# Moving a quarter of the partial groups of an output projection into the norm stages

## The chip, the cores and the metric

The kernel runs on one core of a Trainium2 chip. The metric is the device time of one execution in microseconds (us). Three runs of the kernel before gave 2637.51, 2638.96 and 2642.91 us, a median of 2638.96 us. The engines are called PE (TensorE, the matrix engine), DVE (VectorE), ACT (ScalarE), POOL (GpSimd) and SP (SyncE, which here only issues transfers).

## The reference

The program is a decoder trunk of two layers over 1024 tokens of width 1024, in float32. Cut to what the change touches:

```
for layer in (0, 1):
    hn = rmsnorm(h, ln_mix_pre[layer])
    m  = o @ w_out              # layer 0: o = attention heads (1024 wide)
                                # layer 1: o = y * recurrent scan (1280 wide)
    h  = h + rmsnorm(m, ln_mix_post[layer])
    u  = rmsnorm(h, ln_mlp_pre[layer])
    h  = h + rmsnorm(square(relu(u @ w_up[layer])) @ w_down[layer], ln_mlp_post[layer])
    h  = h + rmsnorm(p[layer] @ w_proj, ple_norm) * sigmoid(h @ w_gate)
```

## The kernel before

**Products.** Each float32 product is done as three matmuls (`mm3`, L153): both operands are split in a high and a low part (`split`, L121: a cast on ACT, then a subtraction on DVE), and high*high, high*low and low*high are summed in PSUM. One block of 128 contraction rows against 512 columns is three matmuls of 128x512. A weight piece of 256 rows x 512 columns (512 KB) is loaded by SP into `wraw`, of which there are two buffers, and split from there into `wA`, `wB` or `wC` tiles (`stage`, L131).

**The output projection** `m = o @ w_out` is cut in two along the contraction. One part is done early, as soon as its rows of `o` exist, in 16 *partial groups*: a group takes one block of 128 tokens (`tb`, 0 to 7) and one half of the output columns (`nh`, 0 or 1), sums 4 contraction blocks (12 matmuls) in layer 0 and 6 (18 matmuls) in layer 1, is copied from PSUM by ACT into a tile `st`, and goes to a DRAM buffer `part[tb]`. In layer 0 the groups (`out_part`, L650) fill gaps of the last attention heads; the list `parts_` (L685) says how many at each step. In layer 1 (`out_partial`, L870, called at the end of the recurrent mixer with `any_bank`) they stand at the mixer's end and take turns on four PSUM banks: two named `tp`, one `mm`, one `av`. After them two rows of `o` are read back from DRAM (`hyD`) and split.

**The norm stage** (`Layer.mix_out`, L929) does the rest. For each token block `out_row` (L953) reads `part[tb]` into a tile `c`, multiplies the other four contraction blocks (24 matmuls, into one of three pairs of PSUM banks), adds the partial on DVE (`a<-sc,c`), and applies both norms. `combine` (L973) then transposes the normed block on PE (8 transposes into the two `tp` banks) and makes from it the operands of a Strassen-like scheme for the first MLP product: for the first four blocks only `B11` and `B21`, for the last four also the sums T1 to T4 and `B22`, with transposes, casts and subtractions on ACT and DVE. T2, T3 and T4 live in three pairs of tiles `x0`, `x1`, `x2` (`extra`, L932), which nothing uses before the second half of the combines. Six halves of the first MLP products ("leads", `None` in the plan) stand between. Below, R0 to R7 are the rows in the order in which they are done, K0 to K7 their combines.

**What sets the order.** The table `plan` (L1011) gives the order in which the steps are written; a scheduler of the framework then orders each engine's instructions by its own model of times. Each engine and each transfer queue works in its order: an instruction that waits holds what stands behind it.

Of the kernel before, what the change touches and what calls it, by code (L numbers as in the profile page):

```python
# [17 lines left out]
P = 128  # L18
# [21 lines left out]
def tile_hybrid_trunk(  # L40
# [283 lines left out]
    def mixer_attention(woD):  # L324
# [8 lines left out]
        with ExitStack() as cx:  # L333
# [319 lines left out]
            def out_part():  # L653
                ws = {}

                def group(nh, tb):
                    if nh not in ws:
                        ws[nh] = [stage_k(attn_w_out[0], 4 + 2 * i, 2, nh * 512, 512) for i in range(2)]
                    acc = bank("mm")
                    tok_group(acc, tb, lambda kb: (ws[nh][(kb - 4) // 2].h[:, kb % 2, :],  # L660
                                                   ws[nh][(kb - 4) // 2].l[:, kb % 2, :]), range(4, KB))
                    st = at.tile([P, 512], F32, name="st", bufs=2)
                    nc.scalar.copy(out=st, in_=acc)
                    nc.scalar.dma_start(out=woD[tb][:, nh * 512:(nh + 1) * 512], in_=st)

                return [lambda nh=nh, tb=tb: group(nh, tb) for nh in range(2) for tb in range(NT)]

            work_of = {b: block_work(order[n + 1]) if n + 1 < len(order) else
                       out_part() + [lambda tb=tb: ple(tb) for tb in range(NT)]
# [12 lines left out]
            ensure(units[0][1])  # L682
            setup_small(at)
            probs = {0: units[0][1].scores(0)}
            parts_ = [4, 3, 4, 4, 2, 2, 2, 1, 1, 1]  # L685
            for i, (blk, hd, g) in enumerate(units):
                work = work_of[blk]

# [178 lines left out]
    FACTOR = {"A11": B11, "A12": B21, "S2": T2, "S1": T1, "S3": T3, "A22": T4, "S4": B22}  # L867
    NLEAD = 3

    def out_partial(wap, kbs, kpairs, part, st_tile, pick_bank):  # L870

        ws = {}

        def group(nh, tb):
            if nh not in ws:
                ws[nh] = [stage_k(wap, r, 2, nh * 512, 512) for r in kpairs]
            acc = pick_bank()
            tok_group(acc, tb, lambda kb: (ws[nh][(kb - kbs[0]) // 2].h[:, kb % 2, :],
                                           ws[nh][(kb - kbs[0]) // 2].l[:, kb % 2, :]), kbs)
            st = st_tile()  # L880
            nc.scalar.copy(out=st, in_=acc)
            nc.scalar.dma_start(out=part[tb][:, nh * 512:(nh + 1) * 512], in_=st)

        return [lambda nh=nh, tb=tb: group(nh, tb) for nh in range(2) for tb in range(NT)]

    def vec(out, a, b, op):
        nc.vector.tensor_tensor(out=out, in0=a, in1=b, op=op)  # L887

# [22 lines left out]
    class Layer:  # L911
# [14 lines left out]
            return h  # L926


        def mix_out(self, wap, kpairs, src, part, order):  # L929
            layer, TA, TB = self.layer, self.TA, 1 - self.TA  # L930
            self.xpool = tc.alloc_tile_pool(name=f"ux{layer}", bufs=1, side="right", reuse_waits="tile")
            extra = [tuple(self.xpool.tile([P, 4, 512], F32R, name=f"x{x}{i}") for x in "hl")  # L932
# [6 lines left out]
            open_psum(f"ps_o{layer}")  # L939
            pairs[0] = 3  # L940
            with tc.tile_pool(name=f"pre{layer}", bufs=1, reuse_waits="tile") as mp:
                wslots.insert(0, (mp, "wBh", "wBl", 1, 1))
                wcount[0] = 0
                w = [[stage_k(wap, r, 2, nh * 512, 512) for r in kpairs] for nh in range(2)]
                gains = [mp.tile([P, D], F32, name="gain", bufs=2) for _ in range(2)]
                bcast_row(gains[0], ln_mix_post[layer:layer + 1, :])
                bcast_row(gains[1], ln_mlp_pre[layer:layer + 1, :])
                ready = {}

                def blocks(t):  # L950
                    return t.rearrange("p (k t) -> p k t", t=P)

                def out_row(tb):  # L953
                    a = mp.tile([P, D], F32, name="a", bufs=3)
                    pt = self.cpool.tile([P, D], F32, name=f"c{2 + tb % 2}", bufs=1)
                    nc.sync.dma_start(out=pt, in_=part[tb])
                    acc = pair_bank()
                    th, j = divmod(tb, 4)
                    sl = slice(j * P, (j + 1) * P)
                    for nh in range(2):  # L960
                        cs = slice(nh * 512, (nh + 1) * 512)
                        for kb in range(4):
                            lh, ll = U(th, kb)
                            mm3(acc[:, cs], lh[:, sl], ll[:, sl], w[nh][kb // 2].h[:, kb % 2, :],
                                w[nh][kb // 2].l[:, kb % 2, :], kb == 0, kb == 3)
                    vec(a, acc, pt, ALU.add)
                    junk = mp.tile([P, 512], F32, name="r").bitcast(BF16)
                    h = self.add_norm(tb, gains[0], a, a, src(tb), junk, mp)
                    nc.sync.dma_start(out=hD[tb], in_=h)
                    rs = rms_row(mp, a, h)  # L970
                    scale_gain(a, h, rs, gains[1])
                    ready[tb] = a

                def combine(tb):
                    n = ready.pop(tb)
                    th, j = divmod(tb, 4)
                    H, L = ([t[x][:, :, j * P:(j + 1) * P] for t in self.comb] for x in range(2))
                    ps = []
                    for kh in range(2):
                        tp = bank("tp")  # L980
                        for q in range(4):
                            kb = kh * 4 + q
                            nc.tensor.transpose(tp[:, q * P:(q + 1) * P], n[:, kb * P:(kb + 1) * P], ident)
                        ps.append(blocks(tp))
                    p1, p2 = ps
                    s = row_tile()
                    s1, s2 = (blocks(s[:, kh * 512:(kh + 1) * 512]) for kh in range(2))
                    if th == TA:
                        split(H[B11], L[B11], p1)
                        nc.scalar.copy(out=s1, in_=p1)  # L990
                        split(H[B21], L[B21], p2)
                        nc.scalar.copy(out=s2, in_=p2)
                        nc.sync.dma_start(out=self.uD[j], in_=s)
                        return
                    nc.sync.dma_start(out=s, in_=self.uD[j])
                    t2, t3 = (blocks(mp.tile([P, 512], F32, name="u", bufs=2)) for _ in range(2))
                    t1, t4 = s1, s2
                    vec(t1, p1, s1, ALU.subtract)
                    split(H[T1], L[T1], t1)
                    nc.scalar.copy(out=t3, in_=p1)  # L1000
                    vec(t2, p2, t1, ALU.subtract)
                    split(H[T2], L[T2], t2)
                    vec(t3, p2, t3, ALU.subtract)
                    split(H[T3], L[T3], t3)
                    vec(t4, s2, t2, ALU.subtract)
                    split(H[T4], L[T4], t4)
                    split(H[B22], L[B22], p2)

                a, b, c = (self.lead_steps(q, mp) for q in range(NLEAD))
                leads = [a[0], a[1], b[0], c[0], b[1], c[1]]  # L1010
                plan = [(out_row, 0), (out_row, 1), (out_row, 2), (combine, 0), (out_row, 3), (combine, 1),  # L1011
                        (out_row, 4), (combine, 2), (out_row, 5), (combine, 3), None, (combine, 4),
                        (out_row, 6), None, (combine, 5), (out_row, 7), None, None, (combine, 6), None,
                        lambda: self.early_sums(mp), (combine, 7), None]
                for step in plan:
                    if step is None:
                        leads.pop(0)()
                    elif callable(step):
                        step()
                    else:  # L1020
                        step[0](order[step[1]])
                del wslots[0]
# [435 lines left out]
    mixer_attention(parts[0])  # L1458

    m = Layer(0, 1, False)  # L1460
    m.mix_out(attn_w_out[0], (0, 2), lambda tb: x[0, tb * P:(tb + 1) * P, :], parts[0], (4, 5, 6, 7, 0, 1, 2, 3))
    m.mlp_and_ple()

    hyD = [dram.tile([P, S], F32, name=f"hyD{n}") for n in range(RB)]

    def rec_out(rp, wap, hyD):
        for f in out_partial(wap, range(2, KB), (2, 4, 6), parts[1],
                             lambda: rp.tile([P, 512], F32, name="st", bufs=2), any_bank):
            f()

    mixer_recurrent(hyD, rec_out)
    for n in range(2):
        t = row_tile()
        nc.sync.dma_start(out=t, in_=hyD[n])
        for th in range(2):
            split(*U(th, 2 + n), t[:, th * 512:(th + 1) * 512])
    m = Layer(1, 0, True)
    m.mix_out(rec_w_out[0], (8, 0), lambda tb: hD[tb], parts[1], (0, 1, 2, 3, 4, 5, 6, 7))
    m.mlp_and_ple()
    close_u()  # L1480
    close_psum()
# [32 lines left out]
```

## Time and profile before

| | us |
|---|---|
| median of 3 runs | 2638.96 |
| the profiled execution | 2638.4 |
| its span | 2636.5 |
| PE busy | 2506.6 (95%) |
| DVE busy | 1667.2 (63%) |
| ACT busy | 1266.5 (48%) |
| POOL busy | 261.5 (10%) |

The mean granted clock of PE was 0.98. PE is busy in 95% of the whole span, but not evenly: in the two stretches that this change concerns, layer 0 from 636 to 750 us and layer 1 from 1814 to 1926 us, it waits for weights, for the norm chain, and for the two transposed banks. The layer-0 attention before the first stretch ends at 635.7 us, and the recurrent mixer's groups run from 1743 to 1814 us. Times in the rows are starts counted from the span's start; a mark such as [2.05 <-ACT row L990] says that the engine had been idle for 2.05 us and what ended that.

### The profile page before, as it was taken

Reading aid. Unit: us, or ns where it says so; the run is one execution under the profiler, and the core shown is the slowest. Engines: PE = TensorE matmul, PEld = TensorE weight load, DVE = VectorE, ACT = ScalarE, POOL = GpSimd, SP = SyncE. Lnnn points to the kernel's source line nnn. Section 1 sums busy time; section 2 is a strip of 40 time slices with the busy share of each in tenths; the row PEclk is TensorE's granted clock in tenths of the full one; section 3 lists DMA queues with packets and bytes.
Section 4 is the critical chain, followed back from the end, with each engine's and each line's share of the span. In section 5 each row is a group of like instructions: output and inputs, shape, how many; then the busy total and the mean of one; then the engine's idle time right before and its main releaser. Section 6 shows DMA issues by size and latency. Waiting matters only on the chain. (4 is left out here: it accounts for less than half of the span.)

```text
span 2636.5 us, 31218 instructions
## 1 busy us (share of the span) xinstructions
PE 2506.6 (95%) x11681; PEld 2042.1 (77%) x11681; DVE 1667.2 (63%) x2089; ACT 1266.5 (48%) x1867; POOL 261.5 (10%) x374
## 2 busy tenths in 40 slices
PE   8899999987899999999999999998899999999999
PEld 7687888875678887788878778877777887888877
DVE  5565666663787455777775555662876546777763
ACT  4454556663544445444444366662644444443431
POOL 1311323311100000000020000000100000000010
PEclk9999999998899999999999999999999999999999
DMA  4746553524656346444444322144655437444443
GB/s 161 204 140 190 167 151 106 158 71 170 227 196 208 134 161 242 161 149 143 144 183 160 128 87 70 56 149 169 231 196 183 150 136 259 156 152 144 164 164 120
DMA packets 231260, 417.92 MB, mean 159 GB/s; under 512 B 17075, under 2 KB 127772, under 8 KB 231108
## 3 DMA queue, kind: packets, MB, share of 16 engines
q1 hardware_dynamic: 199428, 334.64, 39.2%
q10 hardware_dynamic: 22464, 47.72, 5.0%
q0 software_dynamic: 9216, 33.56, 3.3%
q8 instruction: 92, 1.51, 0.2%
q14 instruction: 60, 0.49, 0.1%
HBM read 290.40 MB, written 125.45 MB: 158 GB/s over the span
## 5 line engine op out<-in xcount | busy, mean ns | idle before, releaser
L122 ACT CAST wAh<-wq 128x1024 fp32r<-128x1024 f32 x114 | 119.6, 1049 | 293.2 <-PE k L156 159.6
L123 DVE TENSOR_TENSOR wAl<-wq,wAh 128x1024 fp32r<-128x1024 f32 x114 | 138.9, 1220 | 103.5 <-ACT wAh L122 103.5
L156 PE MATMUL sc<-uh,wAl 128*128 128x512 f32 x464 | 184.7, 398 | 3.9 <-DVE wAl L123 3.9
L154 PE MATMUL sc<-uh,wAh 128*128 128x512 f32 x464 | 185.4, 400 | 2.3 <-ACT row L1079 1.4
L155 PE MATMUL k<-wAl,uh 128*128 128x512 f32 x464 | 183.7, 396 | 3.0 <-DVE wAl L123 3.0
L154 PE MATMUL k<-wAh,uh 128*128 128x512 f32 x464 | 181.0, 396 | 5.8 <-ACT wAh L122 4.2
L155 PE MATMUL sc<-ul,wAh 128*128 128x512 f32 x464 | 184.5, 398 | 0.0
L156 PE MATMUL k<-wAh,ul 128*128 128x512 f32 x464 | 183.5, 396 | 0.0
L123 DVE TENSOR_TENSOR wAl<-wraw,wAh 128x1024 fp32r<-128x1024 f32 (+1 forms) x88 | 109.8, 1248 | 111.2 <-ACT wAh L122 109.3
L896 POOL TENSOR_TENSOR rs<-ms,nhalf 128x1 f32<-128x1 f32 x56 | 59.0, 1059 | 1163.2 <-ACT ms L894 1163.2
L155 PE MATMUL k<-wAl,ul 128*128 128x512 f32 x432 | 171.2, 396 | 1.5 <-DVE wAl L123 1.5
L156 PE MATMUL k<-wAh,uh 128*128 128x512 f32 x432 | 171.3, 397 | 0.3 <-DVE uh L123 0.3
L154 PE MATMUL k<-wAh,ul 128*128 128x512 f32 x432 | 167.9, 395 | 0.8 <-DVE X L887 0.8
L122 ACT CAST wAh<-wraw 128x1024 fp32r<-128x1024 f32 (+1 forms) x88 | 92.1, 1048 | 154.8 <-PE sc L155 52.1
L154 PE MATMUL sc<-xh,wAh 128*128 128x512 f32 x384 | 152.3, 397 | 0.6 <-DVE row L887 0.6
L155 PE MATMUL sc<-xl,wAh 128*128 128x512 f32 x384 | 151.6, 395 | 0.0
L156 PE MATMUL sc<-xh,wAl 128*128 128x512 f32 x384 | 151.0, 395 | 0.0
L154 PE MATMUL mm<-uh,wAh 128*128 128x512 f32 x312 | 128.7, 413 | 9.5 <-ACT st L349 9.4
L122 ACT CAST wAh<-S 128x1024 fp32r<-128x1024 f32 x60 | 63.0, 1050 | 151.3 <-PE k L156 83.5
L409 DVE CUSTOM_DVE_ANT_0 sn<-sc,bias 128x128 f32<-128x128 f32 (+7 forms) x128 | 94.5, 753 | 55.7 <-PE tp L426 18.0
L412 ACT ACTIVATE sn<-sn,nm 128x128 f32<-128x128 f32 (+7 forms) x128 | 99.2, 776 | 58.9 <-DVE nm L409 58.2
L155 PE MATMUL mm<-ul,wAh 128*128 128x512 f32 x312 | 126.1, 404 | 0.0
(423 smaller groups left out, 6727.1 us busy)
## 6 DMA issues: line engine op xcount, KB each, us to landing
c<-hid SPq DMA_DIRECT2D x112, 512.0 KB
hid<-t POOLq DMA_DIRECT2D x48, 512.0 KB, 4.7
wq<-in_mlp_w_up_dram SPq DMA_DIRECT2D x44, 512.0 KB
hid<-row ACTq DMA_DIRECT2D x38, 512.0 KB
wraw<-in_mlp_w_up_dram SPq DMA_DIRECT2D x36, 512.0 KB
wq<-in_mlp_w_down_dram SPq DMA_DIRECT2D x32, 512.0 KB
hD<-row SPq DMA_DIRECT2D x24, 512.0 KB
wraw<-in_attn_w_in_dram SPq DMA_DIRECT2D x22, 512.0 KB
```

What stands on the lines that cost most here:

```text
L122: nc.scalar.copy(out=dst_h, in_=src)
L123: nc.vector.tensor_tensor(out=dst_l, in0=src, in1=f32(dst_h), op=ALU.subtract)
L154: nc.tensor.matmul(dst, lh, rh, start=start, stop=False, skip_group_check=onto)
L155: nc.tensor.matmul(dst, lh, rl, start=False, stop=False, skip_group_check=onto)
L156: nc.tensor.matmul(dst, ll, rh, start=False, stop=stop, skip_group_check=onto)
L409: nc.vector.tensor_tensor_reduce(out=sn[:, :w], in0=sps[:, :w], in1=bias, scale=-1.0, scalar=BIG, op0=ALU.add, op1=ALU.min, accum_out=nm)
L412: nc.scalar.activation(out=sn[:, :w], in_=sn[:, :w], func=AF.Exp, scale=-1.0, bias=nm, accum_out=z)
L896: nc.gpsimd.tensor_tensor(out=rs, in0=ms, in1=nhalf, op=ALU.pow)
```

## The change

In layer 0 four of the 16 groups (columns `nh` = 1, token blocks 0 to 3) are no longer done in the attention but in the norm stage. In layer 1 all 16 are done there: 12 ahead of the rows, and the last four between the rows and combines. The weights of the `nh` = 1 columns go through the same `wraw` ring, but are split into the tiles of T2 and T3 (`extra_unit`); half of the `hyD` rows goes into the tiles of T4. All groups in the stage use only the two `tp` banks. `out_row` is cut into its matmuls (M) and the rest (R), and the plan has steps G for the groups left.

```diff
-    return [lambda nh=nh, tb=tb: group(nh, tb) for nh in range(2) for tb in range(NT)]
+    return [lambda nh=nh, tb=tb: group(nh, tb) for nh in range(2) for tb in range(nh * 4, NT)]
...
-            parts_ = [4, 3, 4, 4, 2, 2, 2, 1, 1, 1]
+            parts_ = [4, 3, 3, 2, 2, 2, 1, 1, 1, 1]
...
-    def out_partial(wap, kbs, kpairs, part, st_tile, pick_bank):
...
-        def mix_out(self, wap, kpairs, src, part, order):
+        def mix_out(self, wap, kpairs, src, part, order, ppairs, hyD=None):
...
+                def part_group(nh, tb, ws):
+                    acc = bank("tp")
+                    tok_group(acc, tb, lambda kb: (ws[(kb - ppairs[0]) // 2].h[:, kb % 2, :],
+                                                   ws[(kb - ppairs[0]) // 2].l[:, kb % 2, :]),
+                              range(ppairs[0], ppairs[-1] + 2))
+                    st = mp.tile([P, 512], F32, name="u", bufs=2)
+                    nc.scalar.copy(out=st, in_=acc)
+                    nc.scalar.dma_start(out=part[tb][:, ncol[nh]], in_=st)
+
+                def extra_unit(i, r):
+                    raw = wpool.tile([P, WE], F32, name="wraw", bufs=2)[:, 0:D].rearrange("p (a n) -> p a n", n=512)
+                    nc.sync.dma_start(out=raw, in_=wap[r * P:(r + 2) * P, ncol[1]]
+                                      .rearrange("(k q) c -> q k c", q=P))
+                    u = W()
+                    u.h, u.l = (t[:, 2 * (i % 2):2 * (i % 2) + 2, :] for t in extra[i // 2])
+                    split(u.h, u.l, raw)
+                    return u
+
+                if hyD:
+                    ws = [stage_k(wap, r, 2, 0, 512) for r in ppairs]
+                    for tb in order:
+                        part_group(0, tb, ws)
+                late = [extra_unit(i, r) for i, r in enumerate(ppairs)]
+                moved = {}
+                if hyD:
+                    for tb in order[:4]:
+                        part_group(1, tb, late)
+                    moved = {(TB, 2 + n): tuple(t[:, n, :] for t in extra[2]) for n in range(2)}
+                    for n in range(2):
+                        t = row_tile()
+                        nc.sync.dma_start(out=t, in_=hyD[n])
+                        for th in (TA, TB):
+                            split(*(moved.get((th, 2 + n)) or U(th, 2 + n)), t[:, ncol[th]])
                 wslots.insert(0, (mp, "wBh", "wBl", 1, 1))
                 wcount[0] = 0
                 w = [[stage_k(wap, r, 2, nh * 512, 512) for r in kpairs] for nh in range(2)]
...
-                def out_row(tb):
-                    a = mp.tile([P, D], F32, name="a", bufs=3)
+                accs = {}
+                def out_mm(tb):
...
+                    accs[tb] = acc, pt
+
+                def out_rest(tb):
+                    a = mp.tile([P, D], F32, name="a", bufs=3)
+                    vec(a, *accs.pop(tb), ALU.add)
...
-                plan = [(out_row, 0), (out_row, 1), (out_row, 2), (combine, 0), (out_row, 3), (combine, 1),
...
+                M, R, K, G = out_mm, out_rest, combine, lambda tb: part_group(1, tb, late)
+                plan = [(M, 0), (R, 0), (M, 1), (R, 1), (M, 2), (R, 2), (M, 3), (K, 0), (R, 3), (G, 4), (M, 4),
...
-    mixer_recurrent(hyD, rec_out)
-    for n in range(2):
...
+    mixer_recurrent(hyD, lambda *a: None)
     m = Layer(1, 0, True)
-    m.mix_out(rec_w_out[0], (8, 0), lambda tb: hD[tb], parts[1], (0, 1, 2, 3, 4, 5, 6, 7))
+    m.mix_out(rec_w_out[0], (8, 0), lambda tb: hD[tb], parts[1], (0, 1, 2, 3, 4, 5, 6, 7), (2, 4, 6), hyD)
```

The scheduled order shows what this does to the engines in three places. First SP's queue at the start of layer 0's norm stage; `wraw<-in_attn_w_out` is a piece of the output projection's weights, `c<-part` a partial read back. Before:

```order
L139 DMA wraw<-in_attn_w_out_dram 128x2x512
L209 DMA gain<-in_ln_mix_post_dram 128x1024
L209 DMA gain<-in_ln_mlp_pre_dram 128x1024
L956 DMA c_7586<-part_4_114 128x1024
L956 DMA c_7634<-part_5_115 128x1024
L139 DMA wraw<-in_attn_w_out_dram 128x2x512 x2
L1059 DMA wraw<-in_mlp_w_up_dram 128x4x256 x3
L956 DMA c_7682<-part_6_116 128x1024
```

And now (L941 is the load in `extra_unit`):

```order
L941 DMA wraw<-in_attn_w_out_dram 128x2x512
L209 DMA gain<-in_ln_mix_post_dram 128x1024
L209 DMA gain<-in_ln_mlp_pre_dram 128x1024
L978 DMA c_7529<-part_4_114 128x1024
L978 DMA c_7577<-part_5_115 128x1024
L139 DMA wraw<-in_attn_w_out_dram 128x2x512 x4
L1086 DMA wraw<-in_mlp_w_up_dram 128x4x256 x3
L978 DMA c_7625<-part_6_116 128x1024
```

The second of two late weight loads stands where the rows' second load stood (the first, further up, took the place of the first); all four loads of the rows now stand behind the reads of the partials.

Second, PE's order in layer 0's norm stage around the transposes of K1 to K3. `tp<-ident,a` are the transposes, `sc<-wAh,uh` and the like the rows' matmuls, `tp<-xh,uh` a group's. Before:

```order
L156 MATMUL sc<-wAh,ul_132 128x512
L154 MATMUL sc<-wAh,uh_131 128x512
L155 MATMUL sc<-wAl,uh_131 128x512
L156 MATMUL sc<-wAh,ul_132 128x512
L983 MATMUL tp<-ident,a 128x128 x24
L154 MATMUL sc<-uh_135,wCh 128x512
L154 MATMUL sc<-wBh,uh_131 128x512
L155 MATMUL sc<-wBl,uh_131 128x512
```

And now:

```order
L156 MATMUL tp<-xh_7477,ul_130 128x512
L1009 MATMUL tp<-ident,a 128x128 x4
L154 MATMUL sc<-wAh,uh_131 128x512
L155 MATMUL sc<-wAl,uh_131 128x512
L156 MATMUL sc<-wAh,ul_132 128x512
L154 MATMUL sc<-wAh,uh_131 128x512
L155 MATMUL sc<-wAl,uh_131 128x512
L156 MATMUL sc<-wAh,ul_132 128x512
L154 MATMUL sc<-wAh,uh_131 128x512
L155 MATMUL sc<-wAl,uh_131 128x512
L156 MATMUL sc<-wAh,ul_132 128x512
L1009 MATMUL tp<-ident,a 128x128 x4
```

K1 to K3 stood together; now 15 of R6's matmuls and a group (G4) stand ahead of K1 and the other nine between its halves, two groups (G5, G6) between K1 and K2, the fourth (G7) between K2 and K3, and row R7 ahead of K4 (in the order before, R6's last matmuls and R7 stood behind K4).

Third, ACT's order at the end of the recurrent mixer in layer 1. `ga` belongs to the last scan, `uh<-row` are casts of the last rows of `o`, L881 and L935 copy a group out of PSUM. Before:

```order
L728 ACTIVATE ga<-ga 128x1024 x2
L881 COPY st<-tp 128x512
L881 COPY st<-mm 128x512
L882 DMA part_0_118<-st 128x512
L882 DMA part_1_119<-st 128x512
L881 COPY st<-tp 128x512
L882 DMA part_2_120<-st 128x512
L122 CAST uh_12345<-row 128x512
L122 CAST uh_12089<-row 128x512
L881 COPY st<-av 128x512
```

And now:

```order
L728 ACTIVATE ga<-ga 128x1024 x2
L122 CAST uh_12353<-row 128x512
L122 CAST uh_12097<-row 128x512
L122 CAST uh_12353<-row 128x512
L122 CAST uh_12097<-row 128x512
L935 COPY u<-tp 128x512 x2
L122 CAST xh_15256<-wraw 128x1024 x2
L122 CAST xh_15260<-row 128x512 x2
L936 DMA part_0_118<-u 128x512
L936 DMA part_1_119<-u 128x512
L935 COPY u<-tp 128x512
```

The first copies stood ahead of the casts of the last rows; now they stand behind them.

## Rows read from the trace of the kernel before

**Rows 1.** Windows; columns: stretch, its length, busy PE, PEld, DVE, ACT, POOL, PEclk, DMA
```profile
541.50:563.00 21.50, 21.50 (x127) 18.60 (x125) 12.48 (x25) 11.89 (x25) 1.85 (x6) 1.00 0.20 65
563.00:600.00 37.00, 25.75 (x137) 21.23 (x135) 25.10 (x67) 21.04 (x56) 7.58 (x19) 0.83 0.19 67
661.00:707.00 46.00, 36.21 (x164) 29.01 (x163) 34.45 (x33) 25.45 (x54) 9.55 (x12) 0.85 0.71 248
707.00:750.00 43.00, 39.89 (x176) 31.69 (x175) 38.11 (x49) 30.25 (x47) 3.48 (x4) 0.96 0.68 224
```

**Rows 2.** Timeline of PE, one layer-0 group; columns: start us, us, engine, line
```profile
542.45 0.47 PE L154 MATMUL mm<-wAh,uh 128*128 128x512 f32 x1
...
545.10 0.39 PE L156 MATMUL mm<-wAh,ul 128*128 128x512 f32 x1
```

**Rows 3.** Timeline of SyncE's queue (SPq), layer-0 norm stage
```profile
638.42 0.43 SPq L139 DMA_DIRECT2D wraw<-in_attn_w_out_dram  x1
...
641.78 4.53 SPq L139 DMA_DIRECT2D wraw<-in_attn_w_out_dram  x2
...
662.09 1.47 SPq L956 DMA_DIRECT2D c<-part  x2
```

**Rows 4.** Timeline of ACT, a weight cast of that stage
```profile
643.60 1.04 ACT L122 CAST wAh<-wraw 128x1024 fp32r<-128x1024 f32 x1 [6.45 <-DMA wraw<-in_attn_w_out_dram]
```

**Rows 5.** Timeline of DVE, that stage
```profile
659.70 1.23 DVE L123 TENSOR_TENSOR wCl<-wraw,wCh 128x1024 fp32r<-128x1024 f32 x1 [5.01 <-ACT wCh L122]
660.84 2.35 DVE L887 TENSOR_TENSOR a<-sc,c 128x1024 f32<-128x1024 f32 x2
...
666.91 1.23 DVE L887 TENSOR_TENSOR a<-sc,c 128x1024 f32<-128x1024 f32 x1 [0.68 <-DMA c<-part]
...
678.96 1.22 DVE L887 TENSOR_TENSOR a<-sc,c 128x1024 f32<-128x1024 f32 x1
...
683.62 1.22 DVE L887 TENSOR_TENSOR a<-sc,c 128x1024 f32<-128x1024 f32 x1
```

**Rows 6.** Timeline of PE, transposes of combine, three of the first five
```profile
682.17 1.29 PE L983 MATMUL tp<-ident,a 128*128 128x128 f32 x8 [2.05 <-ACT row L990]
...
693.17 1.94 PE L983 MATMUL tp<-ident,a 128*128 128x128 f32 x8 [5.10 <-DVE a L181]
...
705.85 1.04 PE L983 MATMUL tp<-ident,a 128*128 128x128 f32 x8
```

**Rows 7.** Timeline of PE, first product after the stage
```profile
749.23 0.50 PE L154 MATMUL sc<-uh,wAh 128*128 128x512 f32 x1 [0.68 <-ACT row L1079]
```

**Rows 8.** Timeline of PE, one layer-1 group
```profile
1765.09 0.40 PE L154 MATMUL mm<-wAh,uh 128*128 128x512 f32 x1
...
1769.30 0.40 PE L154 MATMUL tp<-wAh,uh 128*128 128x512 f32 x1
```

**Rows 9.** Timeline of ACT and its queue, layer-1 groups
```profile
1760.16 0.57 ACT L881 COPY st<-tp 128x512 f32<-128x512 f32 x1
...
1760.76 0.82 ACTq L882 DMA_DIRECT2D part<-st  x2
1762.88 0.59 ACT L881 COPY st<-tp 128x512 f32<-128x512 f32 x1 [1.67 <-DMA part<-st]
...
1769.22 1.15 ACT L122 CAST uh<-row 128x512 fp32r<-128x512 f32 x2 [2.29 <-DVE row L845]
1770.28 0.58 ACT L881 COPY st<-tp 128x512 f32<-128x512 f32 x1
```

**Rows 10.** Timeline of PE, end of the layer-1 groups
```profile
1820.30 1.65 PE L154 MATMUL sc<-wBh,uh 128*128 128x512 f32 x3 [6.75 <-ACT wBh L122]
```

**Rows 11.** Timeline of DVE, first add of layer 1
```profile
1836.56 2.40 DVE L887 TENSOR_TENSOR a<-sc,c 128x1024 f32<-128x1024 f32 x2 [7.28 <-PE sc L156]
```

**Rows 12.** Timeline of PE, layer-1 combine 4
```profile
1882.17 1.04 PE L983 MATMUL tp<-ident,a 128*128 128x128 f32 x8
```

**Rows 13.** Timeline of PE, first product after layer 1's stage
```profile
1925.70 0.50 PE L154 MATMUL sc<-uh,wAh 128*128 128x512 f32 x1 [0.68 <-ACT row L1079]
```

More of the change, by code (lines that the diff above doesn't have):

```diff
@@ L868, in tile_hybrid_trunk @@
     NLEAD = 3
-    def out_partial(wap, kbs, kpairs, part, st_tile, pick_bank):
[L872 to L884, printed above, removed]
     def vec(out, a, b, op):
@@ L941, in mix_out @@
             with tc.tile_pool(name=f"pre{layer}", bufs=1, reuse_waits="tile") as mp:
+                ncol = [slice(nh * 512, (nh + 1) * 512) for nh in range(2)]
+                def part_group(nh, tb, ws):
[29 more added lines that the diff above has]
+                            split(*(moved.get((th, 2 + n)) or U(th, 2 + n)), t[:, ncol[th]])
                 wslots.insert(0, (mp, "wBh", "wBl", 1, 1))
@@ L962, in out_row @@
                         for kb in range(4):
-                            lh, ll = U(th, kb)
+                            lh, ll = moved.get((th, kb)) or U(th, kb)
                             mm3(acc[:, cs], lh[:, sl], ll[:, sl], w[nh][kb // 2].h[:, kb % 2, :],
                                 w[nh][kb // 2].l[:, kb % 2, :], kb == 0, kb == 3)
-                    vec(a, acc, pt, ALU.add)
+                    accs[tb] = acc, pt
+                def out_rest(tb):
+                    a = mp.tile([P, D], F32, name="a", bufs=3)
+                    vec(a, *accs.pop(tb), ALU.add)
                     junk = mp.tile([P, 512], F32, name="r").bitcast(BF16)
@@ L1010, in mix_out @@
                 leads = [a[0], a[1], b[0], c[0], b[1], c[1]]
-                plan = [(out_row, 0), (out_row, 1), (out_row, 2), (combine, 0), (out_row, 3), (combine, 1),
-                        (out_row, 4), (combine, 2), (out_row, 5), (combine, 3), None, (combine, 4),
-                        (out_row, 6), None, (combine, 5), (out_row, 7), None, None, (combine, 6), None,
-                        lambda: self.early_sums(mp), (combine, 7), None]
+                M, R, K, G = out_mm, out_rest, combine, lambda tb: part_group(1, tb, late)
+                plan = [(M, 0), (R, 0), (M, 1), (R, 1), (M, 2), (R, 2), (M, 3), (K, 0), (R, 3), (G, 4), (M, 4),
+                        (K, 1), (R, 4), (G, 5), (G, 6), (K, 2), (M, 5), (R, 5), (G, 7), (K, 3), (M, 6), (R, 6),
+                        None, (K, 4), (M, 7), (R, 7), None, (K, 5), None, None, (K, 6), None,
+                        lambda: self.early_sums(mp), (K, 7), None]
                 for step in plan:
@@ L1460, in tile_hybrid_trunk @@
     m = Layer(0, 1, False)
-    m.mix_out(attn_w_out[0], (0, 2), lambda tb: x[0, tb * P:(tb + 1) * P, :], parts[0], (4, 5, 6, 7, 0, 1, 2, 3))
+    m.mix_out(attn_w_out[0], (0, 2), lambda tb: x[0, tb * P:(tb + 1) * P, :], parts[0], (4, 5, 6, 7, 0, 1, 2, 3), (4, 6))
     m.mlp_and_ple()
     hyD = [dram.tile([P, S], F32, name=f"hyD{n}") for n in range(RB)]
[L1466 to L1469, printed above, removed]
-    mixer_recurrent(hyD, rec_out)
-    for n in range(2):
[L1473 to L1476, printed above, removed]
+    mixer_recurrent(hyD, lambda *a: None)
     m = Layer(1, 0, True)
-    m.mix_out(rec_w_out[0], (8, 0), lambda tb: hD[tb], parts[1], (0, 1, 2, 3, 4, 5, 6, 7))
+    m.mix_out(rec_w_out[0], (8, 0), lambda tb: hD[tb], parts[1], (0, 1, 2, 3, 4, 5, 6, 7), (2, 4, 6), hyD)
     m.mlp_and_ple()
```

## The prediction, made before the changed kernel ran

> **What bounds the kernel now.** I read the windows of the two stages first, then PE's timeline for its waits, and last the queues of ACT, DVE and SP at the places where PE waits.
>
> The windows of layer 0 [rows 1] say where work can be hidden. In the attention's 541.5 to 563.0, where most groups that are taken away stand, PE is busy all the time (21.50 of 21.50), DVE for 12.48 and ACT for 11.89: PE alone is the bound. In the next 37 us PE has 25.75, DVE 25.10 and ACT 21.04: no engine is full, it is a chain from one to the other. In the norm stage there are two halves. From the first add (R0, 660.84) to K4 (705.85) PE has 36.21 of 46.00, so about 10 us of waiting; K1 had waited 2.05 us and K3 5.10 us for ACT and DVE [rows 5, 6]. From 707 to 750 DVE has 38.11 of 43.00 and PE 39.89: both nearly full. The stage ends where the first product after it starts, at 749.23 [rows 7]. In front of R0 the stage waits for weights: a piece issued at 638.42 was cast at 643.60, and ACT had been idle 6.45 us for it [rows 3, 4].
>
> In layer 1 the groups are PE's only work until they end. The rows behind them start at 1820.30, 6.75 us after the last group, released by ACT's cast of `wBh`, and the first three matmuls take 1.65 us, twice a full-speed matmul's spacing [rows 10]. Then the stage runs like that of layer 0: R0 at 1836.56, K4 at 1882.17, next product at 1925.70 [rows 11 to 13].
>
> **Prices.** A layer-0 group is 12 matmuls; its first starts at 542.45 and its last at 545.10, 0.24 us apart [rows 2]: 12 x 0.24 = 2.88 us at most. A layer-1 group is 18 matmuls, and the next group starts 4.21 us after it [rows 8]; 12 of 18 of that is 2.81, and I count 2.8 for layer 0. A copy out of PSUM is 0.57 us; a write of a partial, issued at 1760.76, had freed its tile at 1762.88, so 2.1 us [rows 9]; a read back, issued at 662.09, released its add at 666.91, so 4.8 us [rows 3, 5]. One turn of a `wraw` buffer is 5.18 (load) + 1.04 (cast) + 1.23 (subtraction) = 7.45 us [rows 3 to 5].
>
> **Layer 0, attention.** Four groups leave: 4 x 2.8 = 11.2 us of PE. In the full window that is all gain, up to the point where DVE is late next: it has 12.48 us in 21.50, so at most 9.0 us can go there, and the fourth group was at the edge of the stretch where PE waits anyway [rows 1]. Bounds 0 and 11.2; I take 7, nearer to the upper since PE was full.
>
> **Layer 0, before R0.** Two more 512-KB loads go through the same two `wraw` buffers ahead of the four loads of the rows. In the order they take the first two places, so each of the rows' loads comes a turn later. SP stood 4.53 us in the issue of two loads for a free buffer already [rows 3], so there is no slack: +7.4 us to R0, bounds 0 (both loads land beside the attention) and 7.45. Attention and ring together leave R0 where it was: -7 + 7.4 = +0.4.
>
> **Layer 0, R0 to K4.** It took 45.0 us. Now G4 to G7 (11.2 us) stand among K1 to K3, and R7 (24 matmuls, 5.6 us) ahead of K4. The 10 us of idle time look like room, but the groups use the same two `tp` banks as the transposes: each must wait for the copies and sums of the combine before it, and each transposition for ACT's 0.57-us copy of the group. R4's add, in the order behind G4, now waits for G4's partial to go to DRAM and back: copy 0.57 + write 2.1 + read 4.8 = 7.5 us behind the group. The group itself comes after R6's first 15 matmuls, which need R3's PSUM pair (R3's add stood 18.1 us after R0). So R4's add is not before 18.1 + 1.2 + 15 x 0.23 + 2.8 + 7.5 = 33.1 us after R0; it was 22.8 us after R0 before, and K4 followed it by 22.2 us [rows 5, 6]. Added whole, K4 would be at R0 + 55.3; with PE's extra 11.2 + 5.6 and none of it hidden, at R0 + 61.8. I take 58.7, between: +13.7. Bounds: +6.8 (only what PE's 10 us do not hold, 16.8 - 10) and +16.8.
>
> **Layer 0, behind K4.** R6's last matmuls and R7 no longer stand here (6.7 us of PE), and DVE has four 1.22-us row operations fewer of its 38.11: 38.11 - 4.9 = 33.2, and 1.2 more from K7's last operation to the product: 34.4 instead of 43.4, -9.0. Bounds -4.9 and -10. DVE is then the full engine. Layer 0 in all: 0.4 + 13.7 - 9.0 = +5.1.
>
> **Layer 1, the groups.** Before, four groups could be open at a time, and the first copies were at 1760.16 and 1760.63, ahead of the casts of the last rows, which wait for the scan's product and end at 1770.37 [rows 9]. Now only two `tp` banks serve, and both copies stand behind those casts in ACT's order. The third group can start at 1770.4 + 0.57 = 1771.0. In the old order PE started its seventh group at 1769.30 [rows 8]: the new one is four groups and 1.7 us late, 4 x 4.21 + 1.7 = 18.5. The four groups taken out to the rows save 16.8 of that, so the last group ahead of the rows ends 1.7 us later than the last of all did. Bounds of the loss: 0 (the scheduler's copies come free earlier than their place says) and 21 (one more wait of half a group).
>
> Here the Trainium skill is weighed. Its page "Perfetto Trace Analysis", section "Identifying Performance Opportunities", says that consistent bubbles on the engine that should be saturated can mean too little SBUF or PSUM for the next tile. The trace of before has no place with two banks for the groups, so no row shows it; the ACT rows show only when a bank could be freed. Without that loss the total below would be 18.5 us less, 2630; with it the total stands.
>
> **Layer 1, before R0.** The weights' casts now stand among the groups (three weight loads more, but there is time beside the groups to load them), so the 6.75 us of idle and the slow matmuls after it go: 6.75 + 2.3 = 9 us (2.3 is an estimate: ten matmuls at twice the spacing of 0.23). With the 1.7, R0 at -7.3; bounds -25 (no loss at the groups) and +3.
>
> **Layer 1, R0 to the product.** By the same plan as layer 0, with G at 4.21: +16.8 for four groups and +4 for the waits on banks and on the partial that goes to DRAM and back: K4 at R0 + 66.4 instead of 45.6. Behind K4 35 us instead of 43.5: -8.5. Sum -7.3 + 20.8 - 8.5 = +5.0. The stage's own +12.3 could be +4 (G half hidden in PE's waits) or +17 (nothing gained behind K4 but 4.9).
>
> **Sum.** +5.1 + 5.0 = +10.1 us on the profiled execution's 2638.4 (its span 2636.5 and 1.9 around it), which stands 0.6 us below the median of the runs: 2648.5.
>
> **Rivals.**
> A. The groups fill waits. Mechanism: PE's idle time in the norm stages holds them. For it: about 10 us of idle between R0 and K4 and the waits of 2.05 and 5.10 us [rows 1, 6]. Against: the waits are for the chain through DVE and ACT, which the same groups lengthen. Price, in layer 0: the ring costs nothing, K4 comes 1 us later (11.2 - 10), attention gives 11.2 back: -10. Layer 1: -7.3 for R0, 16.8 - 10 = 6.8 for the groups: about 0. Total 2628. It decides if R4's add is within 24 us of R0 and the rows' weights are cast no later than before. This is the faster side.
> B. Two banks and DRAM cost more: the third layer-1 group waits and each later pair again (21 and not 18.5: +2.5), and K4 is at its upper bound (+3 in layer 0, and as much in layer 1). 2648.5 + 8.5 = 2657.
> C. The attention gives nothing, since its chain of the later windows sets its end (25.75 of 37.00 for PE): +7 on the forecast, 2655.5.
> D. It does not do what it says in the sum: the work is only moved, and both ends meet at no change, 2639.
>
> **Chances.** Forecast 0.45, A 0.22, B 0.15, C 0.10, D 0.08. What a measurement of this kernel can tell from no change is 0.2%, 5.3 us: faster is below 2633.7, slower above 2644.2. Of the forecast's 0.45, whose own range is 2635 to 2658, 0.27 is slower, 0.16 the same, 0.02 faster; A is 0.19 faster and 0.03 the same; B 0.15 slower; C 0.08 slower and 0.02 the same; D 0.07 the same and 0.01 faster. That is faster 0.22, same 0.28, slower 0.50. The range of 2628 to 2661 reaches A's time and past B's, and leaves out what lies beyond both.
>
> **What would show each step.** Attention: its last PE operation some 7 us earlier than 635.7. Ring: the first `a<-sc,c` of layer 0 near 661, with ACT idle twice for `wraw` ahead of it. R4's add about 33 us after R0, released by `c<-part`; K4 about 58.7 us after R0, and DVE without gaps from there. Layer 1: PE idle some 14 us until 1771 (on the old clock), released by ACT's copy of a `tp` bank; R0 some 7 us earlier; K4 66 us after R0. The forecast is wrong if the third layer-1 group starts before 1765, if R0 of layer 0 is much before 661, or if K4 follows R0 as closely as before.

## The result and the profile after

The changed kernel takes 2657.9 us (median of four runs, 2653.85 to 2662.23) against 2639.4 before (four runs). The ratio of the two is 1.0071, with a 95% interval of 1.0055 to 1.0086: 18.7 us slower, between 14.5 and 22.7. The forecast was 10.1 us slower, in a range that holds the measured time. The profiled execution of the changed kernel has a span of 2652.1 us and was the fastest of the four, 15.6 us over the span before.

To see where the time went, both traces are cut at the same events: one of the attention's output transposes ahead of the groups that moved, its last transposes, R0's add, K4's transposes, and the first product with T2, which is the first matmul with `xh` behind the stage (called T2 product below; the prediction's "first product" stands 24 matmuls ahead of it). R0 in a table or a sum means the start of R0's add, K4 the start of K4's transposes. PE before the change, start and length in us, at the attention and then at the two T2 products:

```profile
485.55 0.38 PE L501 MATMUL tp<-ident,ot 128*128 128x128 f32 x2
...
635.38 0.33 PE L513 MATMUL tp<-ident,oq 128*128 128x128 f32 x1 [0.68 <-DVE oq L507]
```

```profile
754.93 0.40 PE L154 MATMUL sc<-xh,wAh 128*128 128x512 f32 x1
...
1931.40 0.40 PE L154 MATMUL sc<-xh,wAh 128*128 128x512 f32 x1
```

And PE after the change: attention, first matmul of the rows, K4, T2 product.

```profile
480.84 0.38 PE L501 MATMUL tp<-ident,ot 128*128 128x128 f32 x2
...
622.56 0.33 PE L513 MATMUL tp<-ident,oq 128*128 128x128 f32 x1 [0.68 <-DVE oq L507]
...
639.14 1.22 PE L154 MATMUL sc<-wBh,uh 128*128 128x512 f32 x2 [16.25 <-ACT wBh L122]
...
709.75 1.03 PE L1009 MATMUL tp<-ident,a 128*128 128x128 f32 x8
...
762.41 0.40 PE L154 MATMUL sc<-xh,wAh 128*128 128x512 f32 x1
```

The end of the attention misleads. It comes at 622.56 and not 635.38, 12.8 us earlier, but at 480.84 the trace is already 4.7 us ahead of the one before, in a stretch where the instructions are the same; executions differ by that much there (an experiment below, with the same order up to that point, has the event at 487.5). What the four groups gave is the difference of the differences: 149.8 us before, 141.7 after, 8.1 us. It is gained where the prediction looked for it: counted from the block at 485.6, DVE's instructions in the two traces are level within 0.2 us up to 540 us, and 7.3 us earlier from 562 to 584 us.

DVE in layer 0 after the change, the adds of R0, R3 and R4, and R7's add and its product with the norm's gain:

```profile
652.84 1.23 DVE L871 TENSOR_TENSOR a<-sc,c 128x1024 f32<-128x1024 f32 x1 [0.64 <-PE sc L156]
...
671.87 1.22 DVE L871 TENSOR_TENSOR a<-sc,c 128x1024 f32<-128x1024 f32 x1
...
688.40 1.22 DVE L871 TENSOR_TENSOR a<-sc,c 128x1024 f32<-128x1024 f32 x1 [1.77 <-DMA c<-part]
...
714.66 1.22 DVE L871 TENSOR_TENSOR a<-sc,c 128x1024 f32<-128x1024 f32 x1
...
718.72 1.22 DVE L871 TENSOR_TENSOR a<-a,gain 128x1024 f32<-128x1024 f32 x1
```

R4's add waits last for the partial (`c<-part`) and comes 35.6 us after R0's, against 22.8 before [rows 5]. With K4 at 709.75, R0 to K4 takes 56.9 us and not 45.0 [rows 5, 6]. R7's add, at 714.66, is still behind K4.

Layer 1, DVE's last scan before the change:

```profile
1765.19 2.28 DVE L837 TENSOR_TENSOR_SCAN row<-a,gx 128x1024 f32<-128x1024 f32 x1
```

The same scan and R0's add after it:

```profile
1774.09 2.28 DVE L837 TENSOR_TENSOR_SCAN row<-a,gx 128x1024 f32<-128x1024 f32 x1
...
1833.23 1.22 DVE L871 TENSOR_TENSOR a<-sc,c 128x1024 f32<-128x1024 f32 x1 [7.65 <-PE sc L156]
```

PE there, the third group, K4 and the T2 product:

```profile
1779.80 0.80 PE L154 MATMUL tp<-wAh,uh 128*128 128x512 f32 x1 [13.68 <-ACT u L935]
...
1900.65 1.04 PE L1009 MATMUL tp<-ident,a 128*128 128x128 f32 x8
...
1946.88 0.39 PE L154 MATMUL sc<-xh,wAh 128*128 128x512 f32 x1
```

PE stood still for 13.68 us for ACT's copy of the first group. On ACT the copies stand behind the casts of the last rows:

```profile
1774.21 1.14 ACT L122 CAST uh<-row 128x512 fp32r<-128x512 f32 x2 [5.04 <-DVE row L845]
1778.13 1.14 ACT L122 CAST uh<-row 128x512 fp32r<-128x512 f32 x2 [2.78 <-DVE row L845]
1779.17 1.06 ACT L935 COPY u<-tp 128x512 f32<-128x512 f32 x2
```

R0 came 59.1 us after the scan and not 71.4 [rows 11], K4 67.4 after R0 and not 45.6 [rows 11, 12], the T2 product 46.2 after K4 and not 49.2. Differences in the table are taken before rounding.

| stretch, us | before | after | difference | forecast |
|---|---|---|---|---|
| attention (from the block at 485.6) | 149.8 | 141.7 | -8.1 | -7 |
| its end to R0 | 25.5 | 30.3 | +4.8 | +7.4 |
| R0 to K4 | 45.0 | 56.9 | +11.9 | +13.7 |
| K4 to T2 product | 49.1 | 52.7 | +3.6 | -9.0 |
| layer 0 | | | +12.2 | +5.1 |
| scan to R0 | 71.4 | 59.1 | -12.2 | -7.3 |
| R0 to K4 | 45.6 | 67.4 | +21.8 | +20.8 |
| K4 to T2 product | 49.2 | 46.2 | -3.0 | -8.5 |
| layer 1 | | | +6.6 | +5.0 |

Both layers together lose 18.8 us, close to the 18.7 of the runs. The profiled spans differ by less since the changed one had a lead of 4.7 us before anything changed, and lost 1.4 between the layers.

### The profile page after: what moved, and what is told of

Its sections match the earlier page's. It is cut to its first block, busy times and chain, and to the rows that moved or that the text cites. A ratio compares the mean times of both kernels' runs of the same rounds, so it can differ in the third digit from the quotient of the medians.

```text
span 2652.1 us, 31224 instructions
## 1 busy us (share of the span) xinstructions
PE 2507.5 (95%) x11681; PEld 2041.6 (77%) x11681; DVE 1672.1 (63%) x2091; ACT 1270.6 (48%) x1869; POOL 260.3 (10%) x374
## 5 line engine op out<-in xcount | busy, mean ns | idle before, releaser
L880 POOL TENSOR_TENSOR rs<-ms,nhalf 128x1 f32<-128x1 f32 x56 | 58.9, 1055 | 1168.9 <-ACT ms L878 1165.5
```

The costliest lines, as they stand in the source:

```text
L880: nc.gpsimd.tensor_tensor(out=rs, in0=ms, in1=nhalf, op=ALU.pow)
```

## The experiments

They take the change apart by layer first, then by the groups' place and banks. Runs of one batch share their runs of the kernel before (medians 2641.0, 2641.3 and 2642.8 us), and ratios are to those.

**The layers by themselves, and the attention alone.** In the first kernel `mix_out` of layer 1 and the recurrent mixer are as before the change, in the second the attention and layer 0's `mix_out` (`None` brings the old plan and groups back). The third leaves the four groups out altogether.

```diff
# layer 0 alone
-    m.mix_out(..., (0, 1, 2, 3, 4, 5, 6, 7), (2, 4, 6), hyD)
+    m.mix_out(..., (0, 1, 2, 3, 4, 5, 6, 7), None)
# layer 1 alone
-    m.mix_out(..., (4, 5, 6, 7, 0, 1, 2, 3), (4, 6))
+    m.mix_out(..., (4, 5, 6, 7, 0, 1, 2, 3), None)
# the attention alone: its groups as in the changed kernel, all else as before the change
-  for nh in range(2) for tb in range(NT)]
+  for nh in range(2) for tb in range(nh * 4, NT)]
-  nc.sync.dma_start(out=pt, in_=part[tb])
+  nc.sync.dma_start(out=pt, in_=part[tb if layer else tb % 4 + 4])
```

Expected of layer 0 alone: 

> The change in layer 0 alone; layer 1 stays as before. Theory: the two layers lose apart from each other, and in the changed kernel's trace the product behind layer 0's norm stage came 7.5 us late. So +7.5 on the kernel before, about 2647, with R0 8 us earlier, K4 57 us after R0 and the product 47 us after K4. Rival: what layer 0 loses is taken up by waits further on, and the loss of 18.5 us is layer 1's: about 2640.

Measured: 2656.6 us, ratio 1.0063 (1.0046 to 1.0080), +16.6. Its trace has the changed kernel's stretches again (30.3, 57.1 and 54.2 us). The rival falls. The loss is larger than the 7.5 expected: that number still had the trace's lead in it, and 12.2 from the table is at the lower end of the interval (12.1 to 21.1).

Expected of layer 1 alone: 

> The change in layer 1 alone; layer 0 and the attention stay as before. Theory: the product behind layer 1's norm stage comes 6.6 us late, so about 2646, with PE waiting 13.7 us for ACT's copy of the third group's bank. Together with the layer-0 run this should add up to 14 us, and 4 us of the 18.5 would be left for stretches that the change does not touch. Rival: the whole loss is here, 2657.

Measured: 2649.0 us, 1.0029 (1.0021 to 1.0038), +7.7, as expected. Scan to R0, R0 to K4 and K4 to the T2 product are 58.9, 64.6 and 47.6. The two runs add up to 24.3 us against 18.7 for the whole change; with some 5 us of uncertainty on the sum and 4 on the whole, that does not tell from plain addition.

Expected of the attention alone: 

> The four layer-0 groups are taken out of the attention and not done anywhere: rows 4 to 7 add another block's partial, read by the same transfers; the norm stages are as before. It prices the attention term alone. Theory from the changed trace (last operation of the attention 12.8 us earlier): 12.8 us less, 2626.6, with the first matmul of the rows 12 us earlier. Rival 1, the prediction's term: 7 us less, 2632. Rival 2: the chain of the attention sets its end, no gain, 2639.

Measured: 2632.6 us, 0.9966 (0.9952 to 0.9980), -9.0. The interval reaches from -12.7 to -5.3, so no gain at all is ruled out and 12.8 just so; the trace agrees. PE at the same two places:

```profile
487.50 0.38 PE L501 MATMUL tp<-ident,ot 128*128 128x128 f32 x2
...
630.04 0.33 PE L513 MATMUL tp<-ident,oq 128*128 128x128 f32 x1 [0.68 <-DVE oq L507]
```

142.5 us against 149.8: 7.3 less. Over all thirteen traces, the four with the old attention have 149.8 to 152.5 us here, the nine with the new one 141.4 to 143.2; the means are 8.9 apart. The prediction's term was right to some 2 us, the 12.8 of the first reading was not.

**Where R6 and R7 stand, and the groups taken out.**

```diff
# R6 and R7 behind K4
-  (G, 7), (K, 3), (M, 6), (R, 6), None, (K, 4), (M, 7), (R, 7), None, (K, 5), None, None, (K, 6)
+  (G, 7), (K, 3), None, (K, 4), (M, 6), (R, 6), None, (K, 5), (M, 7), (R, 7), None, None, (K, 6)
# layer 0 alone, without its groups
-  G = lambda tb: part_group(1, tb, late)
+  G = lambda tb: None
-  nc.sync.dma_start(out=pt, in_=part[tb])
+  nc.sync.dma_start(out=pt, in_=part[tb if layer else tb % 4 + 4])
```

Expected of the rows behind K4: 

> The changed kernel with the matmuls of R6 and R7 written behind K4 again, as before the change; the groups stay where they are. In the changed trace PE is idle 10 us between K4 and the first T2 product behind the stage, since nothing of the rows is left there to cover the copies and casts of the leads. Theory: K4 comes 6 us earlier and the part behind it does not get longer than before the change (49 us), so 6 to 10 us less than the changed kernel, ratio to the kernel before about 1.004. Rival: DVE and ACT set the pace of rows and combines, the idle time only moves ahead of K4 again, ratio 1.007.

Measured: 2664.0 us, 1.0088 (1.0071 to 1.0106): no gain, perhaps a loss. R0 to the T2 product is 105.7 us in layer 0 (109.6 in the changed kernel) and 117.8 in layer 1 (113.6). The theory falls: K4 of layer 0 comes 58.5 us after R0 and not earlier than in the changed kernel (56.9). In layer 0 PE's idle time in the two stretches goes from 2.6 + 9.8 us to 6.7 + 2.1, in layer 1 from 3.7 + 5.7 to 6.5 + 6.9: over both layers it moves ahead of K4 and is not less. Why one layer gains what the other loses is open.

Expected without groups: 

> The change in layer 0 alone, without its four groups in the norm stage: they are not computed (rows 4 to 7 add another block's partial, read by the same transfers); the late loads, the new plan and the shorter attention stay. It prices the groups where they stand. Theory: they cost their full 11.2 us of PE, as the waits around them do not shrink: R0 to the T2 product 98 us and not 109.6, ratio about 1.001 to 1.002. Rival: the new order of rows and combines costs by itself, the groups lie in waits: no more than 4 us less than the layer-0 run, 1.005.

Measured: 2637.2 us, 0.9983 (0.9970 to 0.9997). The windows R0 to K4 and K4 to T2 product (PEclk is PE's granted clock as a share of the full one); columns: stretch, length, busy PE, PEld, DVE, ACT, POOL, PEclk, DMA share, GB/s. Before the change:

```profile
660.84:705.85 45.01, 35.22 (x154) 28.02 (x154) 34.10 (x33) 24.30 (x53) 9.55 (x12) 0.85 0.70 243
705.85:754.93 49.08, 45.97 (x206) 36.73 (x205) 43.18 (x55) 33.70 (x52) 3.48 (x4) 0.97 0.71 238
```

After:

```profile
652.84:709.75 56.91, 54.31 (x248) 43.58 (x247) 37.05 (x35) 28.18 (x59) 10.70 (x13) 1.00 0.60 211
709.75:762.41 52.66, 42.91 (x178) 32.80 (x177) 43.27 (x55) 33.45 (x50) 2.19 (x3) 0.90 0.64 222
```

The change in layer 0 alone:

```profile
656.21:713.27 57.06, 54.27 (x248) 43.59 (x247) 36.73 (x35) 28.16 (x59) 11.68 (x13) 1.00 0.61 209
713.27:767.50 54.23, 44.44 (x177) 34.27 (x176) 44.81 (x56) 34.16 (x51) 2.19 (x3) 0.87 0.64 217
```

And the same without the groups:

```profile
653.75:700.89 47.14, 43.52 (x195) 34.53 (x193) 35.99 (x34) 25.21 (x56) 9.82 (x13) 0.96 0.67 236
700.89:749.71 48.82, 42.84 (x184) 33.60 (x182) 40.50 (x53) 32.70 (x49) 4.23 (x3) 0.93 0.71 228
```

Without groups the two stretches take 96.0 us (98 expected), 1.9 more than they took before. So the groups cost 15.3 us there in the traces (111.3 in the layer-0 run; 13.6 against the changed kernel's 109.6), more than their 11.2 us of PE, and 0.8% by the runs, 21 us (15 to 27). Of the 15.3 us, 12.3 are busy time of PE and 3.0 are idle time on top. PE's idle time did not pay for any of it over the two stretches: 9.8 + 3.1 us before, 3.6 + 6.0 without the groups, 2.6 + 9.8 in the changed kernel. It moved from ahead of K4 to behind it. Behind K4 PE in the changed kernel waits for ACT's copies, for its casts of the leads' weights and for the combine:

```profile
714.09 0.51 PE L154 MATMUL sc<-uh,wCh 128*128 128x512 f32 x1 [3.30 <-ACT c L1123]
...
715.93 1.12 PE L1009 MATMUL tp<-ident,a 128*128 128x128 f32 x4 [1.11 <-ACT u L1026]
...
724.30 0.50 PE L154 MATMUL sc<-uh,wCh 128*128 128x512 f32 x1 [0.90 <-ACT wCh L122]
...
746.69 0.80 PE L154 MATMUL sc<-uh,wAh 128*128 128x512 f32 x1 [2.34 <-ACT wAh L122]
```

And DVE has 55 instructions and 43 us behind K4 before and after the change, so nothing had become shorter there. Counted by name, only one row's add and gain have left that stretch: R6's. R7's are still in it. Two sums for later weights (`wq`) stand in it instead. DVE is idle for 9.4 of its 52.7 us. PE has no matmul of the rows there any more and 28 matmuls fewer in all, but only 3.1 us less of busy time, at a granted clock of 0.90 and not 0.97.

**The weight ring.** In the layer-0 run the late loads go behind the rows' loads:

```diff
-  late = [extra_unit(i, r) for i, r in enumerate(ppairs)]
...
   w = [[stage_k(wap, r, 2, nh * 512, 512) for r in kpairs] for nh in range(2)]
+  late = [extra_unit(i, r) for i, r in enumerate(ppairs)]
```

Expected: 

> The change in layer 0 alone, with the two late weight loads behind the four loads of the rows and not ahead of them. Theory: from the attention's end to R0 25.5 us as before the change, and not 30.3, and the 4.8 us show in the time: against the layer-0 run (ratio 1.0063) about 1.0045. Rival: the late weights then come late for the first group, or the leads' weights come two turns later, and R0 to the product behind the stage gets longer by as much: 1.006.

Measured: 2656.4 us, 1.0058 (1.0042 to 1.0073). The attention's end to R0 is 26.4 us and not 30.3, near what the theory has, but R0 to K4 is 60.1 and not 57.1. From the attention's end to the T2 product 2.9 us are left against the layer-0 run's trace and 1.1 against the changed kernel's. The time does not tell from that of the layer-0 run, 1.3 us less with some 6 either way, so a gain of 4.8 is neither shown nor ruled out. In the changed kernel SP's issue of the four loads shows the ring, 13.04 us long (4.53 for two before [rows 3]):

```profile
628.91 13.04 SPq L139 DMA_DIRECT2D wraw<-in_attn_w_out_dram  x4
```

**The groups' place and their banks.** Three kernels on layer 1: the changed one with the 12 groups ahead of the rows on eight banks; all 16 groups ahead of the rows on eight banks, and on two. `early_bank` gives a `tp` bank on every third call, else one half of a row pair.

```diff
# the changed kernel, its 12 groups ahead of the rows on eight banks
-  part_group(0, tb, ws)
+  part_group(0, tb, ws, early_bank())
-  part_group(1, tb, late)
+  part_group(1, tb, late, early_bank())
# all 16 ahead, early_bank as above; layer 0 and plan as before the change
-  for tb in order[:4]:
-      part_group(1, tb, late)
+  for tb in order:
+      part_group(1, tb, late, early_bank())
# all 16 ahead on two banks (in early_bank)
-  if turn[0] % 3 == 0:
+  if True:
       return bank("tp")
```

Expected on eight banks: 

> The changed kernel, with the 12 layer-1 groups ahead of the rows on eight PSUM banks (the two tp banks and the halves of the three row pairs) and not on two; nothing else. Theory: PE's wait of 13.7 us for the copies goes, and the rows start as much earlier: 2657.9 - 13.7 = about 2644. Rival: the rows' weights or the last recurrent rows are late instead, so less than 5 us is gained, 2653 to 2658.

Measured: 2660.4 us, 1.0077 (1.0065 to 1.0089): no gain. The one wait of 13.7 us has become five of 9.1 in all:

```profile
1787.92 0.50 PE L154 MATMUL sc<-wAh,uh 128*128 128x512 f32 x1 [3.58 <-ACT u L935]
...
1794.59 0.50 PE L154 MATMUL sc<-xh,uh 128*128 128x512 f32 x1 [0.67 <-ACT u L935]
...
1807.47 0.50 PE L154 MATMUL sc<-wBh,uh 128*128 128x512 f32 x1 [0.21 <-ACT u L935]
...
1818.08 0.50 PE L154 MATMUL sc<-wBh,uh 128*128 128x512 f32 x1 [0.67 <-ACT u L935]
...
1823.74 0.80 PE L154 MATMUL sc<-xh,uh 128*128 128x512 f32 x1 [4.01 <-ACT u L935]
```

R0 comes 54.0 us after the scan (59.1), but the T2 product 119.1 after R0 (113.6). I expected the wait to go and the rest to stay; it did not. What is gained ahead of R0 is lost behind K4, 51.4 us against 46.2, where PE's idle time is 8.1 us and not 5.7.

Expected with all groups ahead: 

> Layer 0 as before the change. In layer 1 all 16 groups are done in the norm stage's pools ahead of the rows, on eight PSUM banks, with the nh=1 weights in the tiles of T2 and T3 and the old plan behind. Theory: what the move wins is the idle time and slow clock ahead of the rows (6.75 us and some 2), what it loses is the two banks and the groups among the combines; with both gone 5 to 9 us less than the kernel before, ratio 0.997 to 0.998. Rival: the groups' copies and writes (two tiles) hold PE as in the run on eight banks, no gain, 1.000 or above.

Measured: 2631.8 us, 0.9965 (0.9951 to 0.9978): 9.2 us less than before the change. The windows scan to R0, R0 to K4, K4 to T2 product:

```profile
1766.51:1823.15 56.64, 52.15 (x214) 41.14 (x212) 17.93 (x19) 18.89 (x28) 0.00 (x0) 0.94 0.52 173
1823.15:1874.98 51.83, 47.88 (x214) 38.57 (x215) 34.07 (x32) 26.89 (x57) 9.66 (x12) 0.97 0.67 237
1874.98:1923.04 48.06, 44.33 (x205) 35.44 (x204) 42.08 (x54) 33.90 (x52) 3.97 (x4) 1.00 0.65 209
```

156.5 us against 166.2 before the change and 172.8 after it.

Expected on two banks: 

> The layer-1 run with all 16 groups ahead of the rows, but on the two tp banks alone; layer 0 as before the change. It prices the two banks by themselves. Theory: PE waits some 13.7 us for the first copy again, as in the changed kernel, and the time rises by as much against the run on eight banks (0.9965): 1.0015. Rival: the wait only moves, as in the changed kernel on eight banks, no more than 4 us: 0.998 or below.

Measured: 2649.3 us, 1.0030 (1.0018 to 1.0042), 17 us more than on eight. PE's wait is there again:

```profile
1774.49 0.80 PE L154 MATMUL tp<-wAh,uh 128*128 128x512 f32 x1 [14.22 <-ACT u L935]
```

So the bank term is real, and costs 17 us where nothing else is in the way; and on eight banks the groups among the combines, with the new plan, cost as much (scan to T2 product 173.1 against 156.5). Scan to T2 product: 172.8 us with both, 173.1 with the banks mended, 175.2 with place and plan mended, 156.5 with all mended. Place and plan were not taken apart in layer 1; in layer 0, without groups, R0 to the T2 product takes 1.9 us more with the new plan than with the old one.

**The same in layer 0.**

```diff
# layer 1 and plan as before the change; in the second kernel with layer 1's 16 ahead too
+  for tb in order[4:]:
+      part_group(1, tb, late, early_bank())
```

Expected: 

> Layer 1 as before the change. In layer 0 the four groups are done ahead of the rows, on eight PSUM banks, and the old plan stands behind. In the changed trace PE is idle 16.3 us ahead of the rows while their weights load; the groups' own weights come first. Theory: the groups fill that idle time, and R0 to the T2 product is 94 to 96 us again: attention -8, weight ring +4.8, groups 0 to +3, so -3 to 0, ratio 0.999 to 1.000. Rival: the four groups cost their 11.2 us here too, ratio 1.003 or above.

Measured: 2640.0 us, 0.9987 (0.9977 to 0.9996), -3.4. The groups stand where PE waited 16.25 us for the rows' weights:

```profile
632.59 0.50 PE L154 MATMUL sc<-xh,uh 128*128 128x512 f32 x1 [1.50 <-ACT xh L122]
...
634.60 0.50 PE L155 MATMUL sc<-xl,uh 128*128 128x512 f32 x1 [0.64 <-DVE xl L123]
...
641.16 0.50 PE L155 MATMUL sc<-xl,uh 128*128 128x512 f32 x1 [0.29 <-DVE xl L123]
...
648.25 0.50 PE L154 MATMUL sc<-wBh,uh 128*128 128x512 f32 x1 [0.44 <-ACT u L951]
```

The end of the attention to R0 is 31.5 us, 1.3 more than with no group there, and R0 to the T2 product 94.0.

Expected of both: 

> Both layers with their groups ahead of the rows on eight banks and the old plan behind. Theory: the layers add up: the layer-1 run of this kind (0.9965) and the layer-0 run of this kind, so 0.996 to 0.997, about 9 us less than before the change. Rival: no more than the layer-1 run alone, or less, if layer 0's weights ring costs what the attention gives.

Measured: 2632.5 us, 0.9969 (0.9958 to 0.9981), 8.2 us less than before the change. The two do not add up to more than layer 1 alone; the intervals overlap, so whether layer 0 then still gives something is open. With their groups ahead of the rows on eight banks, layer 0, layer 1 and both layers each beat the kernel before and the changed one.

## Why the prediction was right, and where it was not

- **The attention (-7).** Right: -8.1 in the trace, -8.9 over all traces, -9.0 (-12.7 to -5.3) by the run that does only this. PE was the bound in that window [rows 1], and the gain is made in it.
- **The weight ring (+7.4).** The mechanism was right, the size was not: +4.8. In the run that mends it 3.9 us come back ahead of R0, and 3.0 of them are lost by K4; whether the time gains is not shown.
- **R0 to K4 (+13.7 and +20.8).** Right: +11.9 and +21.8. R4's add was forecast 33.1 us after R0 and came 35.6 after it, released by the partial. PE's idle time ahead of K4 fell from 9.8 to 2.6 us, so there the groups and R7 did fill waits; that over both stretches the groups are paid in full is shown for layer 0 by the run without them; in layer 1 no run takes them out.
- **Behind K4 (-9.0 and -8.5).** This step failed: +3.6 and -3.0. It took four row operations off DVE and 6.7 us off PE, and called DVE the bound there. Only R6's two operations left, R7's add still starts 4.9 us behind K4, and with two weight sums that came in DVE's work did not get less: 55 instructions before and after. Nor was DVE full: it is idle for 9.4 us. The 1.2 us that the sum adds from K7's last operation to the product is in no row. PE's idle time in that stretch went from 3.1 to 9.8 us, and most of it is for copies and casts. That R6 and R7 had been the cover behind K4 was my first explanation; the run that puts them back is 3.9 us shorter in layer 0, 4.1 longer in layer 1 and no faster, so it does not bear it out. Without groups the stretch is 48.8 us with the new plan, and 49.1 with the old one. So without groups the new plan is worth nothing there, and of the forecast's gain of 17.5 us layer 1 has 3.0 and layer 0 none.
- **Two banks in layer 1 (+18.5 against 16.8).** Right in place and size: 13.68 us, until 1779.80, which is 1770.9 on the clock of before (scans 8.9 us apart), forecast 1771.0. By the runs the two banks cost 17 us. The page "Perfetto Trace Analysis" of the Trainium skill, section "Identifying Performance Opportunities", takes a gap that repeats on the engine that should be saturated as a possible sign of too little PSUM for the next tile. The traces agree in part: too few banks made PE wait, but once and not in a repeating gap, 14.22 us in the run that does only this; and more banks alone gave nothing as long as the groups stood among the combines. A run with two banks and the copies ahead of the casts in ACT's order was not made, so how much of the wait is due to that order is not shown.
- **Layer 1 ahead of R0 (-7.3).** The sign was right, -12.2 measured. The forecast counted the idle time and the slow matmuls. Most of the other 5 us can be read from the traces: between the scan and R0's add PE did 57 of the rows' matmuls before and 42 after, which at 0.23 us is 3.5 us. The last group ends 4.7 us later, but 15 of the 42 stand among the groups.

Half of the failed step was hidden by luck: behind K4 the two layers came out 18.1 us worse than forecast, the other steps 9.4 us better (mainly 1.1, 2.6 and 4.9 us ahead of R0). What is left is the miss of 8.7. With the other steps as forecast the time would have been near 2667, beyond the range's 2661. One of the prediction's own signs of being wrong came true: R0 of layer 0, at 652.84, is much before 661; 4.7 of the 8 us are the lead of that execution, the rest is the attention and the ring.

Rival B has the right time, 2657, but not the place: K4 was not at its upper bound, and in layer 1 PE waited once for a bank ahead of R0 and not again. Rival A falls with R4's add 35.6 us after R0 and with the run without groups, rival C with the run of the attention alone.

What stays open: why the run on eight banks gives back behind K4 what it gains ahead of R0, and what sets the pace behind K4, where neither PE nor DVE is full and the groups add idle time (3.0 us of the 15.3).

## What to carry to other kernels

Idle time of an engine in a chain of dependent steps need not be room for work: here the work put among the steps delayed the next one, and the idle time turned up again behind. Look for idle time in which the engine waits for something that the new work doesn't delay, as the loads ahead of the rows: there 11.2 us of groups cost 1.3 (2.1 in the kernel with both layers). And two faults can hide each other: mending the banks alone or place and plan alone gave nothing, and both gave 16 us.

## What the runs showed of the hardware

Executions differ in stretches that no edit touches. Up to the attention's transposes PE, DVE, ACT and POOL have the same instructions in the same order in all thirteen traces; the transposes were at 485.55, 480.84 and 487.50 us in the three shown, and anywhere from 479.9 to 489.3 us in the thirteen. The stretch between the layers, into whose two ends alone the edits reach, took 1010 to 1022 us. A difference of two absolute times is worth no more than that; differences within a stretch, counted from an event near it, agreed with the runs (18.8 and 18.7 us, where the runs are good to 4).
